# One more tile by quarters in the second column half of both feed-forward outputs, and nine DRAM sums made in another stage

## The chip, the core and the metric

The kernel runs on one core of a Trainium2 chip. The metric is the time of one execution in microseconds on the device. The engines are named as in the profile: PE (TensorE: matmuls; PEld is its weight load), DVE (VectorE), ACT (ScalarE), POOL (GpSimd) and SP (SyncE, which issues most of the DMAs).

## What is computed

One decoder layer for 512 tokens of width 1024, in float32: a half-step SwiGLU feed-forward, a token mixer (HGRN2 and mLSTM heads side by side), and a second half-step SwiGLU feed-forward, each between two RMS norms.

```python
def swiglu_ffn(x, w_in, w_out):                     # w_in 1024 x 5632, w_out 2816 x 1024
    gate, up = jnp.split(x @ w_in, 2, axis=-1)
    return (jax.nn.silu(gate) * up) @ w_out
...
x = x + 0.5 * rms_norm(swiglu_ffn(rms_norm(x, norm_pre[l, 0]), ffn1_w_in[l], ffn1_w_out[l]), norm_post[l, 0])
mixed = token_mixer(rms_norm(x, norm_pre[l, 1]), ...)
x = x + rms_norm(mixed, norm_post[l, 1])
x = x + 0.5 * rms_norm(swiglu_ffn(rms_norm(x, norm_pre[l, 2]), ffn2_w_in[l], ffn2_w_out[l]), norm_post[l, 2])
```

The change touches only how the products with `w_out` are formed, for both feed-forwards (`f1`, `f2`), and when their prepared weights are made.

## The kernel before

**Splits.** Every float32 operand of a large product is split in two rounded parts, high and low. ACT makes the high part by a copy (L294 for weights, L884 for activations), DVE the low part by a subtraction (L296, L885). A product is then three matmuls: high by high, high by low, low by high. Weights come from DRAM into the rings `raw` (3 buffers) and `raw2` (5); their split goes to one of four places (`WBUF = 4`) of the tile `w`. `feed` splits ahead for as long as a place is free; `pull` takes the next ready weight, `drop` frees its place. All items stand in one list in the order of use; a load is due up to 8 items ahead.

**Input stage of a feed-forward** (`ffn_in`). 77 products of 24 matmuls of 128 x 256 (L619), 11 tiles of 7 products, with some sums of weights made on DVE (L310; a few in the second one on POOL).

**Output stage** (`ffn_out`). The 2816 rows of `w_out` are 11 tiles `k2` of 256 rows; the 1024 output columns are two halves of 512. The loop goes over the halves, and in each over the tiles in the order `OUT`. A *plain* tile is 48 matmuls of 128 x 256 (L1004). A *quartered* tile (listed in `QUARTERED`) uses a form with seven products in place of eight: 42 matmuls (L1012), into the four accumulators `C` and four further ones `M["p1"]`, `M["p5"]`, `M["p6"]`, `M["p7"]`. Within a quartered tile the order of products is p1, C[1][1], C[1][0] (with the first weight, `w`), then p7, p5, p6, C[0][1] (with the second, `v`).

A quartered tile needs two weights: three quarters of the plain one (a split of 768 columns), and their *sums* (1024 columns), which are made beforehand in DRAM: `sums_ahead` issues three copies on SP's queue (L938 to L940) and then, one call later each, three adding transfers on POOL's queue (L944). `make_sums` advances all sums under way by one step and begins at most one new one (or up to three of those begun early).

It also needs the activations' quarters (`h_quarters`: two copies on ACT, two subtractions on DVE) and their sums (`h_sums`: three subtractions on DVE, L919), and the split of the sums (`s_tile`, into the ring `s` of three places). Tiles that are quartered in both halves keep quarters and sums from the first half; those in `TWICE` make both again in the second. Tiles 5, 7 and 9 (`APART`) share one buffer of `raw` and `gpre` for their quarters and the tile `xn` for their sums; 2, 4, 6 and 8 have places of their own in the activations' tiles `xq`, which plain tile 7 (`LATER`) uses afterwards.

After the last quartered tile of a half, `common` forms four differences from the `M` accumulators (an ACT copy, L1039, and four dependent DVE operations, L969), and `add` adds them to `C` (two DVE operations for each pair, L969 too).

**The end of the second half.** The last `LAST` tiles of the order (4 in `f1`: 0, 1, 7, 5; 2 in `f2`: 0, 1) are held back and run by chunks of 128 tokens (`chunk`, `last`). The first chunk goes tile by tile into `C[0]`, the second goes into `C[1]`, so `add(C, T, 1)` must be done before it, and `add(C, T, 0)` comes after the first. Behind each chunk its norm and residual follow.

**Where the sums of `f2` are made.** 15 sums: seven are begun at the end of `f1` (`EARLY = 7`), and these and the next six (`AHEAD = 13`) go on from calls of `make_sums` inside the mixer's jobs; the last two are made in the first half of `f2`'s output. `f1` makes its 13 sums from every fifth product of its input stage from the fifteenth on (counted from 0, behind the head products), and from every second tile of the first half.

Of the kernel before, what the change touches and what calls it, by code (L numbers as in the profile page):

```python
# [23 lines left out]
PAIRS = NF // 2  # L24
# [60 lines left out]


FIRST = (2, 3, 4, 5, 6, 7, 8, 9)
QUARTERED = {"f1": [FIRST, (2, 3, 4, 6, 8)], "f2": [FIRST, (2, 3, 4, 6, 8, 9, 5)]}
OUT = {"f1": [list(range(PAIRS)), [10, 2, 4, 3, 6, 8, 9, 0, 1, 7, 5]]}
OUT["f2"] = [OUT["f1"][0], [10, 2, 4, 3, 6, 8, 9, 5, 7, 0, 1]]  # L90
LAST, APART, TWICE = {"f1": 4, "f2": 2}, (5, 7, 9), (5, 9)
PLACES, LATER = {2: 1, 4: 2, 6: 0, 8: 3}, {7: (2, 3)}

AGAIN, ROWS = (10,), (18, 19, 20, 21)
EVERY, EARLY, AHEAD = 5, 7, 13

# [27 lines left out]
class Layer:  # L124
    def __init__(self, ctx, tc, aps):
# [717 lines left out]
    def ffn_in(self):  # L843

        nc = self.nc
        if not self.second:
            self.begun = ()
            self.sums_due("f1")
        for n, (p, t) in enumerate(ORDER2[len(HEADS2) :] if self.second else ORDER[len(HEADS) :]):
            if n > 14 and n % EVERY == 0 and not self.second:  # L850
                self.make_sums()
            if n == 14 and self.second:

                with self.behind(self.pooled):
# [12 lines left out]
        self.lag()  # L867
# [96 lines left out]
    def ffn_out(self, gpost_row, scale, after, trans, head):  # L964
# [3 lines left out]
        nc, mm = self.nc, self.nc.tensor.matmul  # L968
        tt = lambda out, a, b, op: nc.vector.tensor_tensor(out, a, b, op=op)  # L969
        f = "f2" if self.second else "f1"  # L970
        OF, QF, LF = OUT[f], QUARTERED[f], LAST[f]
        low = self.low
        seq = [(half, k2) for half in range(2) for k2 in OF[half]]
        made = deque((h, None) for h in self.hs)
# [1 line left out]
        kept, again = {}, deque()  # L976

        def more(n):
            while count[0] < min(n, len(seq)):
                half, k2 = seq[count[0]]  # L980
                count[0] += 1
                if k2 in QF[half]:
                    if k2 not in kept or half and k2 in TWICE:
                        stay = k2 in QF[1] and k2 not in TWICE
                        a = self.h_quarters(k2, PLACES.get(k2))
                        with self.behind(*([] if stay else [low])):
                            kept[k2] = a, self.h_sums(k2, stay)
                    a, f = kept[k2]
                    made.append((a, self.s_tile(f)))
                elif half and k2 in AGAIN:  # L990
                    made.append(again.popleft())
                else:
                    made.append((self.h_tile(k2, self.x_place(*LATER[k2]) if half and k2 in LATER else None), None))
                    if not half and k2 in AGAIN:
                        again.append(made[-1])

        def plain(C, w, h, i, v, begin):

            hi, lo = ([t[:, kk * 512 : (kk + 1) * 512] if len(t.shape) == 2 else t[:, kk] for kk in range(2)] for t in h)
            c = i // 2  # L1000
            out = C[i % 2][v][:, QUARTER * c : QUARTER * (c + 1)]
            for kk in range(2):
                for n, (a, b) in enumerate(((hi, 0), (hi, 1), (lo, 0))):
                    mm(  # L1004
                        out, a[kk][:, i * P : (i + 1) * P], w[:, b, kk, QUARTER * v : QUARTER * (v + 1)],
                        start=begin and c == kk == n == 0, stop=kk == 1 and n == 2, skip_group_check=True,
                    )

        def product(ps, A, B, begin):
            for c in range(2):  # L1010
                for n, (a, b) in enumerate(((0, 0), (0, 1), (1, 0))):
                    mm(  # L1012
                        ps[:, QUARTER * c : QUARTER * (c + 1)], A[a][:, c], B[b],
                        start=begin and c == n == 0, stop=n == 2, skip_group_check=True,
                    )

        def quartered(C, M, a, s, begin, early):

            quarter = lambda t, j: [self.quarters(t[:, b])[j] for b in range(2)]
            A, S = (lambda j: [a[0][j], a[1][j]]), (lambda j: [s[0][j], s[1][j]])  # L1020
            w = self.pull()
            product(M["p1"], A(1), quarter(w, 1), begin)
            product(C[1][1], A(3), quarter(w, 3), False)
            product(C[1][0], S(3), quarter(w, 2), False)
            self.drop(w)
            v, at = self.pull(), (1, 0, 2, 3)
            if early:
                product(C[0][1], A(2), quarter(v, at[3]), False)
            product(M["p7"], S(0), quarter(v, at[0]), begin)
            product(M["p5"], S(1), quarter(v, at[1]), begin)  # L1030
            product(M["p6"], S(2), quarter(v, at[2]), begin)
            if not early:
                product(C[0][1], A(2), quarter(v, at[3]), False)
            self.drop(v)

        def common(M, t):

            p1, q, x, y = t
            nc.scalar.copy(p1, M["p1"])  # L1039
            tt(q, M["p5"], p1, ALU.subtract)  # L1040
            tt(q, M["p6"], q, ALU.add)
# [12 lines left out]

        with self.behind(*([self.loaded] if self.second else [])):
            g = self.gain("gpost", gpost_row)
        if self.second:
            self.sums_due("f2", done=AHEAD)
        n = 0
        for half in range(2):  # L1060
            C = [[self.ps() for _ in range(2)] for _ in range(2)]
            M, T, left = None, None, len(QF[half])
            for m, k2 in enumerate(OF[half][: PAIRS - LF * half]):
                more(n + 2)
                h, sums = made.popleft()
                if sums:
                    begin = M is None
                    if begin:
                        M = {p: self.ps() for p in ("p1", "p5", "p7", "p6")}

                    quartered(C, M, h, sums, begin, half and OF[1][m : m + 2] == list(TWICE)[::-1])
# [135 lines left out]
    def ffn_items(self, name, w_in, w_out):  # L1207
# [570 lines left out]
    def mixer(self):  # L1778
        nc, tc = self.nc, self.tc
        self.got, self.jobs = set(), deque()  # L1780
        self.sums_due("f2", AHEAD, EARLY)
        with tc.tile_pool(name="ma", bufs=1) as ma:
            self.vh = ma.tile([P, NT, NH, P], F32, name="vh")
            self.qk = ma.tile([P, NT, T], F32, name="qk")
# [193 lines left out]
```

## Time and profile before

| What | Value |
|---|---|
| Median of 3 runs (lowest, highest) | 915.06 us (914.81, 915.23) |
| Profiled execution: own time, span | 914.82 us, 913.1 us |
| PE busy | 904.7 us (99% of the span) |
| DVE, ACT, POOL busy | 767.1, 522.3, 183.2 us |
| Mean granted PE clock | 0.999 |
| First feed-forward | from 0 to about 338 us; its output stage from about 223 |
| Mixer | to about 585 us |
| Second feed-forward: input stage, output stage | about 585 to 795, about 795 to the end |

In a group's row the columns are line, engine, operation, output and inputs, shapes and count, then busy time in us and mean ns of one, then the idle time of the engine before them and what ended it. In a timeline's row they are start and length in us, then the instruction; what stands in brackets is the engine's idle time before it and what ended it.

### The profile page before, as it was taken

What the parts mean: (1) busy time and instruction counts of PE and PEld (TensorE: products, weight loads), DVE (VectorE), ACT (ScalarE), POOL (GpSimd) and SP (SyncE); (2) the same over time, 40 slices, a digit from 0 to 9 for tenths busy, and PEclk for the clock granted to TensorE, in tenths of its full rate; (3) what the DMA queues carried; (4) which work ended last, traced back from release to release, by engine and by line L of the source; (5) the groups of instructions that cost most, each with busy time, mean ns of one, the idle gap of its engine ahead of it and who ended that gap; (6) DMA issues with size and microseconds to landing.
All of it is one profiled execution on the core that took longest, in us unless ns stands there. A gap on an engine that the chain in (4) does not pass through costs nothing.

```text
span 913.1 us, 18148 instructions
## 1 busy us (share of the span) xinstructions
PE 904.7 (99%) x7330; PEld 874.7 (96%) x7330; DVE 767.1 (84%) x1005; ACT 522.3 (57%) x749; POOL 183.2 (20%) x256
## 2 busy tenths in 40 slices
PE   9999999999999999999999999999999999999997
PEld 8999999999999999998888888899999999999997
DVE  6899988889888876699986655699899889988886
ACT  7645545557566557857643345694445545757661
POOL 2541112121111047742230300313000000010002
PEclk9999999999999999999999999999999999999999
DMA  9355779775897825899953127053354445388542
GB/s 311 83 161 140 186 191 213 188 156 137 222 273 237 249 62 143 158 200 210 204 119 116 40 76 253 24 162 95 97 156 140 139 130 156 101 238 242 171 144 93
DMA packets 127921, 146.51 MB, mean 160 GB/s; under 512 B 16335, under 2 KB 100303, under 8 KB 127837
## 3 DMA queue, kind: packets, MB, share of 16 engines
q1 hardware_dynamic: 111868, 130.14, 46.8%
q0 software_dynamic: 15680, 14.69, 11.8%
q8 instruction: 57, 0.93, 0.4%
q10 hardware_dynamic: 288, 0.52, 0.2%
q14 instruction: 28, 0.22, 0.1%
HBM read 143.20 MB, written 31.48 MB: 191 GB/s over the span
## 4 chain that ended last, share of the span: by engine, by line
PE 62%; ACT 0%; DVE 0%; DVEq 0%; POOLq 0%; issue 0%; POOL 0%; ACTq 0%
PE ps L619 23%; PE ps L1012 8%; PE ps L549 6%; PE ps L198 5%; PE ps L200 5%; PE ps L199 5%; PE ps L1004 4%; PE ps L560 1%; PE ps L1441 1%; PE ps L364 1%; PE ps L1540 0%; PE ps L1742 0%; PE ps L1491 0%; PE ps L1715 0%; PE ps L1739 0%; PE ps L1505 0%
## 5 line engine op out<-in xcount | busy, mean ns | idle before, releaser
L294 ACT CAST w<-raw 128x1024 fp32r<-128x1024 f32 x246 | 250.9, 1027 | 190.6 <-PE ps L619 91.7
L296 DVE TENSOR_TENSOR w<-raw,w 128x1024 fp32r<-128x1024 f32 x246 | 299.4, 1221 | 30.7 <-ACT w L294 29.5
L619 PE MATMUL ps<-xq,w 128*128 128x256 f32 x2016 | 236.9, 277 | 0.0
L619 PEld LDWEIGHTS ps<-xq,w 128*128 128x128 f32 x2016 | 232.8, 188 | 0.0
L619 PE MATMUL ps<-sq,w 128*128 128x256 f32 x1512 | 177.6, 276 | 0.0
L619 PEld LDWEIGHTS ps<-sq,w 128*128 128x128 f32 x1512 | 174.2, 188 | 0.0
L310 DVE TENSOR_TENSOR raw<-raw,raw 128x1024 f32<-128x1024 f32 x72 | 89.8, 1252 | 7.1 <-DMA raw<-in_ffn_w_in_dram 5.6
L1012 PE MATMUL ps<-w,hs 128*128 128x256 f32 x672 | 80.9, 276 | 0.0
L1004 PE MATMUL ps<-w,hs 128*128 128x256 f32 x672 | 79.2, 276 | 0.0
L1012 PEld LDWEIGHTS ps<-w,hs 128*128 128x128 f32 x672 | 78.3, 188 | 0.0
L1004 PEld LDWEIGHTS ps<-w,hs 128*128 128x128 f32 x672 | 77.5, 188 | 0.0
L198 PE MATMUL ps<-w,xq 128*128 128x512 f32 x176 | 71.1, 404 | 0.0
L200 PE MATMUL ps<-w,xq 128*128 128x512 f32 x176 | 68.9, 392 | 0.0
L199 PE MATMUL ps<-w,xq 128*128 128x512 f32 x176 | 68.6, 390 | 0.0
L944 POOL DMA_DIRECT2D f2sums<-in_ffn_w_out_dram x15 | 20.2, 1522 | 178.6 <-DMA f2sums<-in_ffn_w_out_dram 178.1
L549 PE MATMUL ps<-xq,w 128*128 128x256 f32 x480 | 55.7, 278 | 0.0
L549 PEld LDWEIGHTS ps<-xq,w 128*128 128x128 f32 x480 | 54.9, 188 | 0.5 <-issue 0.5
L884 ACT CAST hs<-hf 128x1024 fp32r<-128x1024 f32 x32 | 33.7, 1053 | 27.4 <-PE ps L1012 19.7
L885 DVE TENSOR_TENSOR hs<-hf,hs 128x1024 fp32r<-128x1024 f32 x32 | 39.1, 1223 | 9.0 <-ACT hs L884 8.4
L944 POOL DMA_DIRECT2D f1sums<-f1sums x26 | 22.0, 847 | 108.6 <-DMA f1sums<-in_ffn_w_out_dram 57.4
L944 POOL DMA_DIRECT2D f2sums<-f2sums x30 | 26.3, 911 | 85.7 <-DMA f2sums<-in_ffn_w_out_dram 44.6
L310 POOL TENSOR_TENSOR raw<-raw,raw 128x1024 f32<-128x1024 f32 x12 | 32.6, 2722 | 40.9 <-DVE w L296 40.7
(263 smaller groups left out, 1234.2 us busy)
## 6 DMA issues: line engine op xcount, KB each, us to landing
raw<-in_ffn_w_in_dram SPq DMA_DIRECT2D x98, 512.0 KB, 4.7
raw<-in_ffn_w_out_dram SPq DMA_DIRECT2D x44, 512.0 KB, 5.5
raw<-in_w_mix_in_dram SPq DMA_DIRECT2D x28, 512.0 KB, 4.7
raw<-f2sums SPq DMA_DIRECT2D x15, 512.0 KB, 5.1
raw<-f1sums SPq DMA_DIRECT2D x13, 512.0 KB, 6.4
raw<-in_w_mix_out_dram SPq DMA_DIRECT2D x8, 512.0 KB, 4.3
f2sums<-in_ffn_w_out_dram SPq DMA_DIRECT2D x30, 128.0 KB, 4.9
f2sums<-in_ffn_w_out_dram SPq DMA_DIRECT2D x15, 256.0 KB, 6.4
```

The lines of the kernel that those rows point to most:

```text
L198: mm(ps, sh, mh, start=start, stop=False, **kw)
L199: mm(ps, sh, ml, start=False, stop=False, **kw)
L200: mm(ps, sl, mh, start=False, stop=stop, **kw)
L294: nc.scalar.copy(hi, raw)
L296: self.low = nc.vector.tensor_tensor(lo, raw, hi.bitcast(F32), op=ALU.subtract)
L310: added = (nc.vector if late else nc.gpsimd).tensor_tensor(o, o, c, op=ALU.add)
L549: mm(ps[:, u0:u1], w[:, a, k, :], self.xop(k, b, u0, u1), start=k + n + m == 0, stop=k == ND - 1 and n == 2, skip_group_check=True,)
L619: self.nc.tensor.matmul(ps[:, c], wb[b][:, k, v], left[d][:, k, :], start=first and a + n + k == 0, stop=n == 2 and k == KH - 1, skip_grou ...
L885: self.nc.vector.tensor_tensor(lo, src, hi.bitcast(F32), op=ALU.subtract)
L944: nc.gpsimd.dma_start(to[:, a:b], v, accum_op=ALU.add)
L1004: mm(out, a[kk][:, i * P : (i + 1) * P], w[:, b, kk, QUARTER * v : QUARTER * (v + 1)], start=begin and c == kk == n == 0, stop=kk == 1 and ...
L1012: mm(ps[:, QUARTER * c : QUARTER * (c + 1)], A[a][:, c], B[b], start=begin and c == n == 0, stop=n == 2, skip_group_check=True,)
```

## The change

- In the second half, `f1` also takes tile 9 by quarters (6 quartered tiles in place of 5), and `f2` also tile 7 (8 in place of 7).
- The order of the second half becomes 10, 9, 2, 4, 3, 6, 8, 0, 1, 7, 5 in `f1` and 10, 9, 2, 5, 4, 7, 3, 6, 8, 0, 1 in `f2`. So in both the last quartered tile (8) stands directly ahead of the tiles that are held back; before, the plain tile 9 (`f1`) or 7 (`f2`) stood between.
- Tile 9's quarters and sums are kept from the first half in both. `f2` makes those of 5 and 7 again (before: 5 and 9). The rule that moved the product into C[0][1] forward when 9 and 5 were neighbours is gone.
- `f2`'s sums other than the seven early ones, now nine, are made from its own input stage, at every fifth product from the tenth on. `f1` too begins at the tenth product in place of the fifteenth, and makes 14 sums.

```diff
-QUARTERED = {"f1": [FIRST, (2, 3, 4, 6, 8)], "f2": [FIRST, (2, 3, 4, 6, 8, 9, 5)]}
-OUT = {"f1": [list(range(PAIRS)), [10, 2, 4, 3, 6, 8, 9, 0, 1, 7, 5]]}
-OUT["f2"] = [OUT["f1"][0], [10, 2, 4, 3, 6, 8, 9, 5, 7, 0, 1]]
-LAST, APART, TWICE = {"f1": 4, "f2": 2}, (5, 7, 9), (5, 9)
+QUARTERED = {"f1": [FIRST, (2, 3, 4, 6, 8, 9)], "f2": [FIRST, (2, 3, 4, 6, 8, 9, 5, 7)]}
+OUT = {"f1": [list(range(PAIRS)), [10, 9, 2, 4, 3, 6, 8, 0, 1, 7, 5]]}
+OUT["f2"] = [OUT["f1"][0], [10, 9, 2, 5, 4, 7, 3, 6, 8, 0, 1]]
+LAST, APART, TWICE = {"f1": 4, "f2": 2}, (5, 7, 9), {"f1": (), "f2": (5, 7)}
...
-            self.sums_due("f1")
+        self.sums_due(*(("f2", None, EARLY) if self.second else ("f1",)))
...
-            if n > 14 and n % EVERY == 0 and not self.second:
+            if n > 9 and n % EVERY == 0:
                 self.make_sums()
...
-                    if k2 not in kept or half and k2 in TWICE:
-                        stay = k2 in QF[1] and k2 not in TWICE
+                    if k2 not in kept or half and k2 in two:
+                        stay = k2 in QF[1] and k2 not in APART
...
-            if early:
-                product(C[0][1], A(2), quarter(v, at[3]), False)
             product(M["p7"], S(0), quarter(v, at[0]), begin)
             product(M["p5"], S(1), quarter(v, at[1]), begin)
             product(M["p6"], S(2), quarter(v, at[2]), begin)
-            if not early:
-                product(C[0][1], A(2), quarter(v, at[3]), False)
+            product(C[0][1], A(2), quarter(v, at[3]), False)
...
-        if self.second:
-            self.sums_due("f2", done=AHEAD)
...
-        self.sums_due("f2", AHEAD, EARLY)
+        self.sums_due("f2", EARLY, EARLY)
```

More of the change, by code (lines that the diff above doesn't have):

```diff
@@ L87 @@
 FIRST = (2, 3, 4, 5, 6, 7, 8, 9)
-QUARTERED = {"f1": [FIRST, (2, 3, 4, 6, 8)], "f2": [FIRST, (2, 3, 4, 6, 8, 9, 5)]}
-OUT = {"f1": [list(range(PAIRS)), [10, 2, 4, 3, 6, 8, 9, 0, 1, 7, 5]]}
-OUT["f2"] = [OUT["f1"][0], [10, 2, 4, 3, 6, 8, 9, 5, 7, 0, 1]]
-LAST, APART, TWICE = {"f1": 4, "f2": 2}, (5, 7, 9), (5, 9)
+QUARTERED = {"f1": [FIRST, (2, 3, 4, 6, 8, 9)], "f2": [FIRST, (2, 3, 4, 6, 8, 9, 5, 7)]}
+OUT = {"f1": [list(range(PAIRS)), [10, 9, 2, 4, 3, 6, 8, 0, 1, 7, 5]]}
+OUT["f2"] = [OUT["f1"][0], [10, 9, 2, 5, 4, 7, 3, 6, 8, 0, 1]]
+LAST, APART, TWICE = {"f1": 4, "f2": 2}, (5, 7, 9), {"f1": (), "f2": (5, 7)}
 PLACES, LATER = {2: 1, 4: 2, 6: 0, 8: 3}, {7: (2, 3)}
 AGAIN, ROWS = (10,), (18, 19, 20, 21)
-EVERY, EARLY, AHEAD = 5, 7, 13
+EVERY, EARLY = 5, 7
 FREE = (2, 3, 0, 1)
@@ L970, in ffn_out @@
         f = "f2" if self.second else "f1"
-        OF, QF, LF = OUT[f], QUARTERED[f], LAST[f]
+        OF, QF, LF, two = OUT[f], QUARTERED[f], LAST[f], TWICE[f]
         low = self.low
@@ L1015, in product, with quartered @@
                     )
-        def quartered(C, M, a, s, begin, early):
+        def quartered(C, M, a, s, begin):
             quarter = lambda t, j: [self.quarters(t[:, b])[j] for b in range(2)]
@@ L1069, in ffn_out @@
                         M = {p: self.ps() for p in ("p1", "p5", "p7", "p6")}
-                    quartered(C, M, h, sums, begin, half and OF[1][m : m + 2] == list(TWICE)[::-1])
+                    quartered(C, M, h, sums, begin)
                     left -= 1
```

## The prediction

> **What bounds the kernel now.** I read the page's busy shares first, then the matmul engine's waits, then the chain that ended last, and only then the order of work on DVE where the change touches it.
>
> ```profile
> span 913.1 us, 18148 instructions
> PE 904.7 (99%) x7330; PEld 874.7 (96%) x7330; DVE 767.1 (84%) x1005; ACT 522.3 (57%) x749; POOL 183.2 (20%) x256
> PE ps L194 <- POOL ones L172: 1.2, 1, 1.2
> PE ps L364 <- DVE xn L754: 0.5, 1, 0.5
> PE ps L619 <- ACT xq L384: 0.2, 1, 0.2
> ```
>
> PE is busy for 904.7 of 913.1 us, and all its listed waits together are 1.9 us. A busy PE need not be a fast one, so the chain gives the rate. Its columns are the start, the length and what ran.
>
> ```profile
> 802.81 5.44 PE ps L1004 x48
> 808.25 38.08 PE ps L1012 x336
> 846.33 10.88 PE ps L1004 x96
> 857.21 33.32 PE ps L1012 x294
> 890.53 16.33 PE ps L1004 x144
> 907.03 0.38 ACT junk L453
> ```
>
> These are the second feed-forward's output. L1004 is a plain tile of 48 matmuls, 5.44 us; L1012 a tile by quarters of 42, and eight of them take 38.08 us, 4.76 each. Both come to 0.1133 us a matmul, with no gap between tiles. So PE is packed, a matmul taken away is worth 0.1133 us, and nothing that frees another engine can give time back. The end behind the last matmul (907 to 913) is untouched. The profiled execution took 914.82 us (1.72 outside the span); the median of 915.06 lies 0.24 above it, and I apply the sum to the median.
>
> **The matmuls.** Tile 9 of the first feed-forward and tile 7 of the second go from plain to quartered in the second half: 2 x 6 x 0.1133 = 1.36 us less. By this alone 913.7. The quotient 38.08/336 is steady, so I give this term no range beyond 0.05.
>
> **What the two tiles add elsewhere.** Each brings a second weight load (512 KB) and its split, and the first one its made sum. A kept tile needs only the split of its sums, as long as the plain tile's own split. In the second feed-forward 7's quarters and sums are made again, and 9's no longer: they cancel.
>
> ```profile
> 872.75 0.92 ACT L884 CAST once<-hf 128x256 fp32r<-128x256 f32 x2
> 884.35 1.02 DVE L885 TENSOR_TENSOR once<-hf,once 128x256 fp32r<-128x256 f32 x2
> 285.44 0.95 DVE L296 TENSOR_TENSOR w<-raw,w 128x768 fp32r<-128x768 f32 x1
> 857.05:890.40 33.35, 33.35 (x297) 33.35 (x296) 27.58 (x30) 22.16 (x25) 0.00 (x0) 1.00 0.52 158
> ```
>
> The net on DVE is one split of 0.95 us per feed-forward. In the last row (length, then busy time of PE, its weight loads, DVE, ACT, POOL, then clock, DMA share, GB/s) DVE is busy 27.58 of 33.35 us: 5.8 us free, which covers it. If that cover went, each would cost at most its 0.95. Dropping the early C[0][1] product costs nothing: 9 and 5 are no longer neighbours, and tile 2's 4.76 us lies between, against the 0.92 + 1.02 us of quarters (before, they had to fit behind 9's own products).
>
> **The end of the first feed-forward's second half.** Here I see the one real price. Before, plain tile 9 stood between the last quartered tile (8) and the four tiles of the last loop (0, 1, 7, 5), and its 5.44 us covered DVE's work. After, 8 stands directly ahead of that loop.
>
> ```profile
> 309.52 8.32 PE L1004 MATMUL ps<-w,hs 128*128 128x256 f32 x72
> 319.04 2.88 PE L1004 MATMUL ps<-w,hs 128*128 128x256 f32 x24
> 310.00 1.04 ACT L294 CAST w<-raw 128x1024 fp32r<-128x1024 f32 x1
> 316.12 1.04 ACT L294 CAST w<-raw 128x1024 fp32r<-128x1024 f32 x1
> 309.23 0.68 DVE L969 TENSOR_TENSOR hf<-ps,hf 128x512 f32<-128x512 f32 x1
> 309.83 1.22 DVE L885 TENSOR_TENSOR xq<-hf,xq 128x1024 fp32r<-128x1024 f32 x1
> 310.96 0.69 DVE L969 TENSOR_TENSOR hf<-ps,hf 128x512 f32<-128x512 f32 x1
> 311.56 1.22 DVE L296 TENSOR_TENSOR w<-raw,w 128x1024 fp32r<-128x1024 f32 x1
> 314.43 0.69 DVE L969 TENSOR_TENSOR hf<-ps,hf 128x512 f32<-128x512 f32 x1
> 315.03 1.29 DVE L969 TENSOR_TENSOR ps<-ps,hf 128x512 f32<-128x512 f32 x2
> 316.25 1.23 DVE L885 TENSOR_TENSOR hs<-hf,hs 128x1024 fp32r<-128x1024 f32 x1
> 317.40 1.22 DVE L296 TENSOR_TENSOR w<-raw,w 128x1024 fp32r<-128x1024 f32 x1
> ```
>
> DVE ran without a gap from 308 to 318.6, and its last split (tile 5's weights) was done 0.5 us ahead of its use (tile 5 begins at 319.04). In a row of them a split holds DVE for 1.14 us (309.83 to 310.96) and a difference for 0.60. In the same clock, tile 8 now runs from 309.52 to 314.28. Its place for tile 7's weights frees after 18 matmuls, at 311.56; ACT starts 0.2 to 0.5 us later (before: freed 309.52, started 310.00), so DVE can take that split at about 312.85. From there it owes, before the second chunk may start: that split 1.14, four differences 2.5 (the first needs M[p5], done at 312.9), the low parts of 7 and 5 and of 5's weights 3.4 (7's low part and 5's weights lie in places that 8 holds until 314.28), and the first sum into C[1] 0.65: 7.7 us, to 320.55. PE would come there at 314.28 + 5.44 = 319.72. So 0.8 us of waiting. The best order (sums at once, x and y behind) leaves 0.4; with tile 5's low part late (needed at 318.6, done at 320.0 if a difference goes ahead of it twice) 1.4. I take 0.8, the order in which ready work is taken as in the rows.
>
> **The same place in the second feed-forward.** The last loop has two tiles, so only 24 x 0.1133 = 2.72 us cover it.
>
> ```profile
> 890.61 1.48 DVE L969 TENSOR_TENSOR hf<-ps,hf 128x512 f32<-128x512 f32 x2
> 892.13 0.69 DVE L969 TENSOR_TENSOR hf<-hf,ps 128x512 f32<-128x512 f32 x1
> 892.85 0.69 DVE L969 TENSOR_TENSOR hf<-ps,hf 128x512 f32<-128x512 f32 x1
> ```
>
> Dependent differences follow each other every 0.74 us. Tile 8 would end at 857.21 + 38.08 = 895.29, M[p5] is done 1.36 earlier, and by then DVE has finished the splits of 0 and 1 (the later place frees when 8 starts, 890.5; 0.5 + 1.04 on ACT and 1.14 on DVE end at 893.2). Four differences from 893.95 end at 896.9, the first sum into C[1] at 897.6, and PE comes for it at 898.0. Slack 0.4, so I take 0. If tile 1's low part (1.14) falls behind the differences, it is 0.7; that end stays in the range.
>
> **The nine sums.** Six leave the mixer, two leave the first half of the second feed-forward's output, and tile 7's is new; all nine are made from its input stage. Each is three copies on SP's queue and three adding transfers on POOL's.
>
> ```profile
> 340.00:585.00 245.00, 244.90 (x1570) 217.83 (x1569) 181.78 (x326) 138.78 (x206) 83.02 (x127) 1.00 0.59 143
> 60.00:230.00 170.00, 170.00 (x1499) 170.00 (x1498) 153.59 (x171) 92.47 (x117) 28.51 (x30) 1.00 0.73 183
> 600.00:795.00 195.00, 195.00 (x1719) 195.00 (x1719) 181.73 (x194) 108.82 (x140) 11.41 (x4) 1.00 0.42 127
> L944 POOL DMA_DIRECT2D f1sums<-f1sums x20: 805/812/1325, 75.5 to 224.1; - x20
> raw<-in_ffn_w_in_dram SPq DMA_DIRECT2D x28, 512.0 KB, 5.6
> raw<-in_ffn_w_in_dram SPq DMA_DIRECT2D x40, 512.0 KB, 3.6
> ```
>
> What leaves the mixer frees nothing, since PE is busy 244.90 of 245.00 us there. Where they go (600 to 795), POOL is busy 11 of 195 us and DMA at 0.42, so 27 transfers of 0.81 to 1.33 us (median and maximum of the row), 22 to 36 us on POOL, lie beside PE; what queues behind them there is nothing that PE waits for. The first feed-forward's input stage (60 to 230) already makes ten sums so, at DMA 0.73, with PE busy 170.00 of 170.00. There a weight load lands in 5.6 us against 3.6 (median): the price is 2.0 us a load. The copies stand ahead of loads on SP, which mostly waits for DVE to free a place anyhow. Is 2.0 hidden?
>
> ```profile
> 643.38 1.23 DVE L310 TENSOR_TENSOR raw<-raw,raw 128x1024 f32<-128x1024 f32 x1 [2.12 <-DMA raw<-in_ffn_w_in_dram]
> 653.20 1.22 DVE L296 TENSOR_TENSOR w<-raw,w 128x1024 fp32r<-128x1024 f32 x1
> 650.12 11.10 PE L619 MATMUL ps<-xq,w 128*128 128x256 f32 x96
> ```
>
> The stage is tightest here, behind a load that came 2.12 us late. Counting splits against products, the split at 653.20 feeds the third product of the last row (24 x 0.1133 = 2.72 each, so from 655.56), which needs the low part after 16 matmuls, at 657.4; ready at 654.4. That is 3.0 us in hand, so 2.0 more is hidden. The one sum slot more in the first feed-forward's input stage and its 14th sum go by the same rows: nothing.
>
> Sum: -1.36 + 0.8 + 0 + 0 = -0.56, to 914.5 (914.26 against the profiled execution's own 914.82).
>
> **Rivals.** *All is hidden* (25%): the low parts fall so that PE never waits; 913.7. For it: PE never waited here so far. Against: 0.5 us in hand before, with 5.44 us of cover. *The last loop's order goes badly* (12%): DVE takes the sums ahead of tile 5's low part and weights, as in the rows from 314.43 to 317.40. Then 5's weights end at 321.4 against 318.5: 2.9 us, 916.6. *The second tail waits too* (6%): 0.7 to 1.1 more, 915.4. *Weight loads starve the second input stage* (8%), which ends slower: the adding transfers and copies share the engines with the loads. It decides from a lateness of 3.0 us at 655.
>
> ```profile
> DMA to landing us min/median/max: 3.7/5.6/9.8
> ```
>
> This row is of the weight loads from 60 to 230. A load at its maximum is 9.8 - 3.6 = 6.2 us late, 3.2 over what is in hand: 914.5 + 3.2 = 917.7. Against it: in that very stage PE lost nothing. The Trainium skill ("DMA: Bandwidth & Descriptors", Queues, rings and completion order) states that each DMA engine takes turns between the queues with work, a packet at a time; a load that shares with one other queue throughout would take twice as long, an estimate of 7.2 us, and by that sum 0.6 us would show and the time be 915.1. The 5.6 us agrees in direction and is less. *A gain beyond the matmuls* (4%): 913.0, if matmuls elsewhere ran closer; no wait in the list offers it.
>
> **How the numbers follow.** The forecast (0.4 to 1.4 us lost at the first tail, 914.1 to 915.1) has 45%. The range runs from a little under the full gain to the bad order, 913.4 to 916.6, and leaves out the starving and the unexplained gain, 12%. A measurement of this kernel tells about 0.2% from no change, 1.8 us: under 913.2 is faster (5%), over 916.9 slower (the starving, and the bad order with one more loss, 11%), the rest 84%.
>
> **What the profile after would show.** L1012 has 84 matmuls more and L1004 96 fewer. Right: around 318 to 320 a PE wait on DVE (hs, w or ps L969) of about 0.8 us, none near 898, none from 640 to 795, POOL's f2sums transfers spread over that stage, weight loads there landing in 5 to 6 us. Wrong, if PE shows no wait by 320 (913.7), or waits on w or raw in the second input stage, or if the second tail's sums come later than its second chunk.

## The result, and the profile after

| | before | after |
|---|---|---|
| Median (lowest to highest) of runs beside each other | 914.81 us (914.33 to 915.23) | 923.88 us (921.82 to 924.41) |
| Ratio, 95% interval | | 1.0094, 1.008 to 1.0109 |
| Profiled execution: own time, span | 914.82, 913.1 us | 922.97, 921.3 us |

The change made the kernel 9 us slower: the forecast was 914.5, the range ended at 916.6. The profiled executions differ by 8.15 us, and these two are compared below. Lines of the page after that answer to those of before:

```profile
span 921.3 us, 18162 instructions
PE 906.4 (98%) x7318; PEld 875.7 (95%) x7318; DVE 765.9 (83%) x1007; ACT 523.6 (57%) x751; POOL 191.5 (21%) x262
L619 PE MATMUL ps<-sq,w 128*128 128x256 f32 x1512 | 179.6, 278 | 5.3 <-DVE ps L638 5.3
L310 DVE TENSOR_TENSOR raw<-raw,raw 128x1024 f32<-128x1024 f32 x72 | 89.7, 1250 | 19.7 <-DMA raw<-in_ffn_w_in_dram 18.4
```

The same two groups, and then the weight loads of the second input stage, before and after:

```profile
L619 PE MATMUL ps<-sq,w 128*128 128x256 f32 x1512 | 177.6, 276 | 0.0
L310 DVE TENSOR_TENSOR raw<-raw,raw 128x1024 f32<-128x1024 f32 x72 | 89.8, 1252 | 7.1 <-DMA raw<-in_ffn_w_in_dram 5.6
```

```profile
raw<-in_ffn_w_in_dram SPq DMA_DIRECT2D x40, 512.0 KB, 3.6
```

```profile
raw<-in_ffn_w_in_dram SPq DMA_DIRECT2D x40, 512.0 KB, 4.8
```

The 12 matmuls are gone (7330 to 7318), and yet the span is 8.2 us longer. L619 has the new wait: PE stood 5.3 us in the input stages' matmuls, waiting for the PSUM subtraction of L638 on DVE. L310 has what stood ahead of it there: the weight additions, before which DVE waited 18.4 us for loads in place of 5.6.

I set the starts of the same matmuls of both traces beside each other. The second input stage begins 0.60 us later than before and ends 8.79 later, so **8.19 us were lost in that stage**; the first feed-forward's end lost its gain (below), and the second output stage won its 0.68 with no wait, as forecast. The waits of PE in the second input stage, by the timeline (start, length, what; in brackets the idle time before):

```profile
689.80 1.98 PE L619 MATMUL ps<-xq,w 128*128 128x256 f32 x16
693.88 3.06 PE L619 MATMUL ps<-sq,w 128*128 128x256 f32 x24 [2.10 <-DVE ps L638]
...
738.54 5.60 PE L619 MATMUL ps<-xq,w 128*128 128x256 f32 x48
747.39 4.32 PE L619 MATMUL ps<-sq,w 128*128 128x256 f32 x24 [3.25 <-DVE ps L638]
751.55 2.88 PE L619 MATMUL ps<-xq,w 128*128 128x256 f32 x24
```

At 0.1133 us a matmul the product of 693.88 should have begun at 691.61 and that of 747.39 at 743.98: 2.27 and 3.41 us. Both are p6, of tiles 4 and 6; p6 adds into a place that DVE fills by subtracting from p5's result, and p5 comes only one other product earlier (2.72 us). The second wait has a tail: the 24 matmuls from 747.39 took 4.16 us in place of 2.72, at half clock. These are 7.1 of the 8.19; most of the rest, about 0.8, is a slower pace of the matmuls behind the first wait (last section).

Behind the first wait, the chain of the kernel after, in order of time, and DVE's queue over the same stretch:

```profile
675.05 7.75 DMA raw<-in_ffn_w_in_dram
...
691.90 1.22 DVE w L296
693.12 0.62 DVE ps L638
693.74 0.14 issue
693.88 8.73 PE ps L619 x72
```

```profile
682.89 1.22 DVE L310 TENSOR_TENSOR raw<-raw,raw 128x1024 f32<-128x1024 f32 x1 [4.40 <-DMA raw<-in_ffn_w_in_dram]
684.03 1.22 DVE L296 TENSOR_TENSOR w<-raw,w 128x1024 fp32r<-128x1024 f32 x1
...
690.76 1.22 DVE L310 TENSOR_TENSOR raw<-raw,raw 128x1024 f32<-128x1024 f32 x1
691.90 1.22 DVE L296 TENSOR_TENSOR w<-raw,w 128x1024 fp32r<-128x1024 f32 x1
693.04 0.69 DVE L638 TENSOR_TENSOR ps<-ps,hf 128x512 f32<-128x512 f32 x1
```

DVE stood 4.40 us for one load that took 7.75, and then worked without a gap until the subtraction at 693.04. It is not that the subtraction stood directly behind the late load: nine instructions lie between, and DVE never had the time to catch up. At the second wait of PE it is the same (the wait of 3.94 below). DVE's longest wait, at 754.93, has no wait of PE behind it:

```profile
737.24 1.23 DVE L310 TENSOR_TENSOR raw<-raw,raw 128x1024 f32<-128x1024 f32 x1 [3.94 <-DMA raw<-in_ffn_w_in_dram]
...
746.55 0.69 DVE L638 TENSOR_TENSOR ps<-ps,hf 128x512 f32<-128x512 f32 x1
...
754.93 1.22 DVE L310 TENSOR_TENSOR raw<-raw,raw 128x1024 f32<-128x1024 f32 x1 [4.83 <-DMA raw<-in_ffn_w_in_dram]
```

By 754.93 PE itself was 8.8 us behind, so the 4.83 us cost nothing more.

### The profile page after: what moved, and what is told of

Read it like the earlier page. It is cut to its first block, busy times and chain, and to the rows that moved or that the text cites. A ratio compares the mean times of both kernels' runs of the same rounds, so it can differ in the third digit from the quotient of the medians.

```text
span 921.3 us, 18162 instructions
## 1 busy us (share of the span) xinstructions
PE 906.4 (98%) x7318; PEld 875.7 (95%) x7318; DVE 765.9 (83%) x1007; ACT 523.6 (57%) x751; POOL 191.5 (21%) x262
## 3 DMA queue, kind: packets, MB, share of 16 engines
q0 software_dynamic: 16800, 15.73, 12.8%
## 4 chain that ended last, share of the span: by engine, by line
PE 45%; DVE 8%; DMA 4%; issue 4%; ACT 1%; POOL 1%; DVEq 0%; POOLq 0%; ACTq 0%
PE ps L1012 8%; PE ps L619 7%; PE ps L549 6%; PE ps L198 5%; PE ps L200 5%; PE ps L199 5%; DMA raw<-in_ffn_w_in_dram 4%; DVE w L296 4%; PE ps L1004 4%; DVE raw L310 2%; PE ps L560 1%; PE ps L1436 1%; POOL raw L310 1%; DVE ps L638 1%; PE ps L364 1%
## 5 line engine op out<-in xcount | busy, mean ns | idle before, releaser
L294 ACT CAST w<-raw 128x1024 fp32r<-128x1024 f32 (+1 forms) x248 | 252.2, 1026 | 194.5 <-PE ps L619 79.7
L296 DVE TENSOR_TENSOR w<-raw,w 128x1024 fp32r<-128x1024 f32 (+1 forms) x248 | 301.2, 1218 | 29.7 <-ACT w L294 28.2
L619 PE MATMUL ps<-xq,w 128*128 128x256 f32 x2016 | 237.2, 277 | 0.0
L619 PEld LDWEIGHTS ps<-xq,w 128*128 128x128 f32 x2016 | 233.2, 188 | 0.0
L619 PE MATMUL ps<-sq,w 128*128 128x256 f32 x1512 | 179.6, 278 | 5.3 <-DVE ps L638 5.3
L619 PEld LDWEIGHTS ps<-sq,w 128*128 128x128 f32 x1512 | 176.0, 189 | 5.8 <-issue 5.7
L310 DVE TENSOR_TENSOR raw<-raw,raw 128x1024 f32<-128x1024 f32 x72 | 89.7, 1250 | 19.7 <-DMA raw<-in_ffn_w_in_dram 18.4
L1012 PE MATMUL ps<-w,hs 128*128 128x256 f32 x720 | 86.5, 276 | 0.0
L1012 PEld LDWEIGHTS ps<-w,hs 128*128 128x128 f32 x720 | 83.8, 188 | 0.0
L944 POOL DMA_DIRECT2D f1sums<-f1sums x28 | 24.3, 868 | 111.0 <-DMA f1sums<-in_ffn_w_out_dram 54.5
L310 POOL TENSOR_TENSOR raw<-raw,raw 128x1024 f32<-128x1024 f32 x12 | 32.6, 2722 | 40.9 <-DVE w L296 40.7
L200 PEld LDWEIGHTS ps<-w,xq 128*128 128x128 f32 x176 | 33.0, 188 | 7.5 <-DVE xq L371 0.3
```

The costliest lines, as they stand in the source:

```text
L200: mm(ps, sl, mh, start=False, stop=stop, **kw)
L294: nc.scalar.copy(hi, raw)
L296: self.low = nc.vector.tensor_tensor(lo, raw, hi.bitcast(F32), op=ALU.subtract)
L310: added = (nc.vector if late else nc.gpsimd).tensor_tensor(o, o, c, op=ALU.add)
L619: self.nc.tensor.matmul(ps[:, c], wb[b][:, k, v], left[d][:, k, :], start=first and a + n + k == 0, stop=n == 2 and k == KH - 1, skip_grou ...
L944: nc.gpsimd.dma_start(to[:, a:b], v, accum_op=ALU.add)
```

## The experiments

Each kernel was timed beside the kernel before (914.46 to 915.13 in these sets). "Stage lost" below is, as above, what the second input stage lost against the profile of before by its matmuls' starts.

**Which part of the change.** The first kernel puts the second feed-forward's sums back where they were, the second moves only them.

```diff
 # the kernel after, sums as before
-        self.sums_due(*(("f2", None, EARLY) if self.second else ("f1",)))
+        if not self.second:
+            self.sums_due("f1")
...
-            if n > 9 and n % EVERY == 0:
+            if n > 9 and n % EVERY == 0 and not self.second:
...
+        if self.second:
+            self.sums_due("f2", done=13)
...
-        self.sums_due("f2", EARLY, EARLY)
+        self.sums_due("f2", 13, EARLY)
```

> The changed kernel, but the second feed-forward's sums are made where they were before (seven and six in the mixer, the last three in the first half of its own output stage). Theory 'place of the sums': the whole loss of the second input stage (8.2 us at the matmuls) comes from making nine sums there; it goes, no PE wait between 590 and 800 us, and what is left is -1.36 us for the two quartered tiles and about +1.1 us lost at the end of the first feed-forward: 914.5 us (914.0 to 915.0). Rival 'the tiles': the new order and the quartered tiles disturb the schedule wherever the sums are made; the time stays at 920 to 924 us.

```diff
 # the kernel before, only the sums moved
-            self.sums_due("f1")
+        self.sums_due(*(("f2", None, EARLY) if self.second else ("f1",)))
...
-            if n > 14 and n % EVERY == 0 and not self.second:
+            if n > (9 if self.second else 14) and n % EVERY == 0:
...
-        self.sums_due("f2", AHEAD, EARLY)
+        self.sums_due("f2", EARLY, EARLY)
```

> The kernel before, with only the place of the second feed-forward's sums changed: its eight sums other than the early seven are made from its input stage, at every fifth product from the tenth on. Theory 'place of the sums': PE waits of 2 to 4 us on DVE appear near 690 and 740 us and the time is 921 to 925 us (8 sums in place of 9; the same mechanism). Rival 'the tiles': 914.8 us, no wait.

Sums put back: 915.58 us (915.02 to 916.7), ratio 1.0009 (1.0 to 1.0018). Sums alone: 925.74 (924.82 to 927.93), ratio 1.0119 (1.0106 to 1.0133), with PE's waits on L638 at the same two products, 5.7 us in all. The place of the sums carries the loss; the quartered tiles have almost no part in it. Both times lie above what was expected: 915.58 is 0.6 over the end of its range, 925.74 is 0.7 over. In the first kernel's profiled execution the second input stage still lost 1.0 us without a listed wait of PE; nearly all of it is the slower pace of the last section.

**The second feed-forward's eighth quartered tile alone** (order and tile as in the change, sums as before, first feed-forward untouched):

```diff
-QUARTERED = {"f1": [FIRST, (2, 3, 4, 6, 8)], "f2": [FIRST, (2, 3, 4, 6, 8, 9, 5)]}
+QUARTERED = {"f1": [FIRST, (2, 3, 4, 6, 8)], "f2": [FIRST, (2, 3, 4, 6, 8, 9, 5, 7)]}
...
-OUT["f2"] = [OUT["f1"][0], [10, 2, 4, 3, 6, 8, 9, 5, 7, 0, 1]]
+OUT["f2"] = [OUT["f1"][0], [10, 9, 2, 5, 4, 7, 3, 6, 8, 0, 1]]
```

> The kernel before with only the second feed-forward's eighth quartered tile and its order (10, 9, 2, 5, 4, 7, 3, 6, 8, 0, 1), the sums made where they were; the first feed-forward as before. The forecast's second-tail term (no wait near 898): 915.0 - 0.68 = 914.3 us. If that tail waits after all: 915 to 915.5 us.

914.45 us (913.63 to 914.97), ratio 0.9993 (0.9984 to 1.0003); the last matmul comes 0.51 us sooner than in the profile of before. The 0.68 is there, and too small to be told from no change.

**Copies or adding transfers.** One kernel has the nine sets of copies in the stage and no adding transfers (they go to a spare place in DRAM; the sums are made as before). One makes the copies in the mixer, and holds the adding transfers in the stage behind a small POOL copy.

```diff
 # the kernel before, and nine sets of copies
+            if n > 9 and n % EVERY == 0 and n < 55 and self.second:
+                to = self.dram.tile([P, 4, QUARTER], F32, name=f"spare{k2}")
...
+                    nc.sync.dma_start(to[:, 0], q[:, 0, 1])
+                    nc.sync.dma_start(to[:, 1], q[:, 1, 0])
+                    nc.sync.dma_start(to[:, 2:], q[:, 1])
```

> The kernel before, with nine sets of the three copies added on SP's queue in the second input stage (into spare DRAM that nobody reads), at every fifth product from the tenth on, and no adding transfers. If copies alone make the loads late: PE waits on DVE before p6 of tiles 4 and 6, 919 to 925 us. If it takes the adding transfers: 914.5 to 916 us.

```diff
 # the kernel after, copies in the mixer, adding transfers in the stage
+                if self.second:
+                    self.mark = nc.gpsimd.tensor_copy(self.col(), self.written)
...
-            with self.behind(*([self.selected] if f == "f2" else [])):
+            with self.behind(*([getattr(self, "mark", self.selected)] if f == "f2" else [])):
...
+            self.copy_more()          # in the mixer's jobs: the three copies of one sum
```

> The changed kernel with the copies of the nine sums issued in the mixer, and the adding transfers held in the second input stage: on POOL each round of them stands behind a small copy of a column that the stage has just written, at every fifth product. If the copies on SP's queue (ahead of weight loads, 0.5 MB a sum) make the loads late, the waits at p6 go and the time is 914 to 916 us. If the adding transfers alone do it, the loss stays at half or more: 918 to 924 us.

Copies: 917.33 us (916.01 to 919.88), ratio 1.0029 (1.0019 to 1.0038). Adding transfers: 918.69 (916.58 to 920.37), 1.0038 (1.0026 to 1.0051), which is 3.1 over the kernel with the sums as before. Together they cost 8.3 (923.88 less 915.58), more than 2.3 and 3.1 added. Neither expectation holds: copies alone lie between the two ranges named for them, and the adding transfers alone are within their 918 to 924, but at 3.1 well under half of the loss.

Two earlier tries at this missed their aim. With the copies in the mixer and nothing to hold the adding transfers back, these too were ordered into the mixer; POOL waited there in order, and PE stood for 29.5 us at one place. With the copies issued on POOL's queue, POOL made them in the kernel's first 60 us, where PE's first products then waited.

```diff
 # copies early
+            self.copy_more()          # in the mixer's jobs
 # copies on POOL
+            on = nc.gpsimd if f == "f2" and not early else nc.sync
+            on.dma_start(to[:, 0], q[:, 0, 1])
```

> The changed kernel, but the three copies of each of the nine sums are issued in the mixer; only the adding transfers stay in the second input stage. 'Copies' (they stand ahead of weight loads on SP's queue, and share the DMA engines with them): weight loads land in 3.6 to 4.5 us, no PE wait in the stage, 914.5 us. 'Any transfer' (the adding transfers on POOL's queue are about half of the bytes and alone hold up the loads): about half the loss stays, 917 to 920 us.

> The changed kernel, but the copies of the nine sums made in the second input stage are issued from POOL's queue and not from SP's: the same bytes at about the same time, and no copy ahead of a weight load on SP's queue. 'Queue order' (the 1.8 us that three copies hold SP, ahead of the loads, is what makes them late): the loss goes, 914.5 us. 'Traffic' (copies and adding transfers take the engines' time while loads are under way): the loss stays, 919 to 924 us.

They took 945.39 and 926.49 us, ratios 1.0331 and 1.0134. In both, none of the nine sums' transfers is left in the second input stage; PE had no wait there, the stage lost nothing, and the loads landed in 3.7 us (median).

**The distance from p5 to p6, and the spacing of the sums.**

```diff
 # the kernel after, p5 of tiles 4, 9 and 6 moved two or three products forward
+for _t in (4, 9):
+    ORDER2.remove(("p5", _t))
+    ORDER2.insert(ORDER2.index(("p1", _t)) + 1, ("p5", _t))
-for _s, _t in ((2, 3), (6, 7), (7, 8)):
+for _s, _t in ((2, 3), (9, 6), (6, 7), (7, 8)):
```

> The changed kernel, with the product p5 of tiles 4, 9 and 6 of the second input stage moved two to four products forward, so that DVE's subtraction, which p6 starts from, has that much more time; the sums stay in the stage. Theory 'short lead': PE loses time only where p6 follows p5 by one other product (2.72 us), and weights have more in hand; with the lead the waits before p6 of 4, 9 and 6 go and the time is 914.3 to 916 us, loads as late as before. Rival 'starved': late loads hold up the weights themselves; PE then waits elsewhere in the stage (on w), 919 to 924 us.

```diff
 # the kernel after, a sum at every seventh product
-            if n > 9 and n % EVERY == 0:
+            if n > 9 and (n % 7 == 3 if self.second else n % EVERY == 0):
```

> The changed kernel with the second feed-forward's nine sums made at every seventh product of its input stage, always at the same place of a tile of seven products, in place of every fifth. The traffic is the same, spread over 7/5 of the time. Theory (lost DVE time: each load that lands late holds DVE, and the lateness adds up when the sums follow each other closely): the loss falls by more than in proportion, to 917 to 920. Rival (each set of copies and adding transfers costs what it costs, nine sets, 8.3 us, wherever they stand): 922 to 924. Second rival (only the place beside p5 and p6 counts, and seven falls onto or beside it every time): under 916, or over 925.

With p5 earlier: 920.44 us (915.88 to 925.64), ratio 1.0066 (1.0041 to 1.009). The waits at p6 of 4 and 6 were gone, but others came. Its timeline of PE (lines of the program 4 later, L623 is L619 and L642 L638):

```profile
698.41 5.72 PE L623 MATMUL ps<-sq,w 128*128 128x256 f32 x48 [1.62 <-ACT ps L674]
755.73 1.19 PE L623 MATMUL ps<-xq,w 128*128 128x256 f32 x8 [0.50 <-DVE w L300]
788.37 3.07 PE L623 MATMUL ps<-sq,w 128*128 128x256 f32 x24 [1.48 <-DVE ps L642]
```

The three stand at p3 of tile 4, p4 of tile 6 and p6 of tile 10, whose p5 was not moved; only 0.50 us is a wait for a weight (w), so neither the theory nor its rival holds. The short way from p5 to p6 is where most of the loss came out, not what made it. The times spread widely, and some 4 us of the profiled execution (923.8) were lost behind the stage, to the slower pace of the last section; so 920.44 is not a clean measure of the lead. With every seventh product: 920.36 (918.94 to 921.88), ratio 1.0063 (1.0051 to 1.0075), stage lost 4.3. Eight of the nine sets of copies and 23 of the 27 adding transfers fall in the stage here, all of them in the kernel after; this traffic, thinner, costs a little over half (4.8 against 8.3 over the kernel with the sums as before). 920.4 lies a little above the 917 to 920 of the theory and well under the 922 of its rival.

**DVE's time by itself.** The additions moved to POOL, and DVE stalled with no traffic at all:

```diff
 # the kernel after, additions of tiles 4 to 9 on POOL
-                late = out[1] >= (HEAD if out[0] == "f1" else 1)
+                late = out[1] >= (HEAD if out[0] == "f1" else 1) and (out[0], out[1]) not in ON_POOL
```

> The changed kernel with the weight additions of tiles 4 to 9 of the second input stage made on POOL in place of DVE (about 24 of 1.25 us; POOL takes 2.72 for one). Theory: the loss is DVE's queue standing behind additions that wait for a late load, so that the PSUM subtraction behind them, which the product p6 starts from, comes late. With those additions on POOL, DVE has 30 us more in the stage and does not wait there for loads: PE's waits on that subtraction go, and the time falls to 915.5 to 918. Rival: the weights themselves are late, whoever adds them. Then PE waits on w in place of the subtraction, POOL's longer additions and the adding transfers queue behind each other, and the time stays at 921 or goes above 924.

```diff
 # the kernel before, four idle reductions on DVE, of 1024, 640, 928 and 1024 columns by 4
+                        with self.behind(self.low):
+                            stall = nc.vector.tensor_reduce(
+                                self.col(4), self.xs[:, :, : STALLS[self.adds_made]], axis=mybir.AxisListType.X, op=ALU.add
+                            )
```

> The kernel before, with four DVE instructions that do nothing for the result (sums over rows of the residual) put ahead of four weight additions of the second input stage, the ones that waited longest for their loads in the changed kernel: some 4.3, 2.7, 3.9 and 4.3 us, 15 us together, against 13 us more of waiting for loads there. No transfer is added, so every load lands as before (3.6 us median). The planner knows of these four when it orders the stage. Theory one (DVE has no time to spare in this stage, so any 13 to 15 us lost there costs PE): waits of PE on the PSUM subtraction as in the changed kernel, and 919 to 924. Theory two (what costs is the lateness that the written order doesn't know of, with the subtraction standing behind it; the same time planned for is worked around): no wait over 0.5 us, 914.5 to 916.5. Rival to both (the loads and transfers themselves slow PE, DVE's waiting is only a companion): 915 and no wait either; it is told from theory two by the matmuls' pace alone.

Additions on POOL: 957.55 us (955.65 to 965.65), ratio 1.0479 (1.0451 to 1.0506), above 924 as the rival had it, though it named no such size. POOL's additions queued behind adding transfers that waited for one another. The waits of PE, of DVE and of ACT (each: us in total, times, longest; lines 1 later here):

```profile
PE ps L620 <- DVE ps L639: 30.8, 6, 10.1
PE ps L620 <- ACT w L295: 1.5, 1, 1.5
PE ps L620 <- DVE w L297: 1.2, 3, 0.6
```

```profile
DVE w L297 <- ACT w L295: 49.5, 8, 13.3
```

```profile
ACT w L295 <- POOL raw L311: 61.9, 9, 15.0
```

DVE now waited hardly for loads (3.5 us) but for ACT's splits, and ACT for weights that POOL had not added yet. Still PE's waits were on the PSUM subtraction (30.8 us), hardly on weights (2.7): whatever DVE waits for, PE feels it through what queues behind. Half of the expectation was right (the queueing on POOL, no gain), half wrong (the name of PE's wait). It doesn't tell whether DVE without that wait would have been quick enough.

The stalls alone tell more: 923.64 us (921.12 to 925.04), ratio 1.0085 (1.007 to 1.01), the loss of the whole change. Its waits, loads and timeline (lines 10 later: L629 is L619, L648 L638):

```profile
PE ps L629 <- DVE ps L648: 5.4, 2, 3.5
```

```profile
raw<-in_ffn_w_in_dram SPq DMA_DIRECT2D x40, 512.0 KB, 3.6
```

```profile
684.54 4.42 DVE L316 TENSOR_REDUCE col<-xs 128x4 f32<-128x4096 f32 x1
688.87 1.22 DVE L320 TENSOR_TENSOR raw<-raw,raw 128x1024 f32<-128x1024 f32 x1
...
694.00 0.70 DVE L648 TENSOR_TENSOR ps<-ps,hf 128x512 f32<-128x512 f32 x1
```

The loads land in 3.6 us as before, no transfer is added, and PE waits at p6 of the same tiles for the same subtraction, 5.4 us against 5.3 in the kernel after. The planner (what fixes the order of each engine's instructions before the kernel runs) knew of these four and gave DVE another order in the stage than before, and PE waits all the same; in the kernel after, whose loads come late, DVE's order there is that of before. So it isn't a matter of an order that was surprised: DVE hasn't the time. Two things stay open. The stalls came with another order, so their loss isn't that of the lost time alone; and no run kept the traffic and took DVE's waits for it away.

The kernels side by side; the second and third column are from 600 to 795 or 800 (median landing of a weight load; DVE's waits for loads, and the longest). Each row is one profiled execution, up to 1.7 us off its kernel's median, and the last column holds the half clock and the slower pace of the last section too:

| Kernel | landing | DVE waits for loads | stage lost |
|---|---|---|---|
| before | 3.6 | 5.6 (2.1) | 0 |
| after, sums as before | 3.6 | 4.6 (2.6) | 1.0 |
| copies alone | 3.7 | 7.9 (3.6) | 2.1 |
| adding transfers alone | 4.6 | 10.4 (3.2) | 5.1 |
| after, every seventh | 4.9 | 13.0 (4.3) | 4.3 |
| sums alone | 5.1 | 16.5 (7.3) | 10.5 |
| after | 4.8 | 18.4 (4.8) | 8.2 |
| before, stalls alone | 3.6 | 6.1 (2.7), and 15.6 of stalls | 10.4 |

**The first feed-forward's tail.** Three tiles held back in place of four, so that plain tile 0 covers the differences (the kernel with the sums as before otherwise):

```diff
-LAST, APART, TWICE = {"f1": 4, "f2": 2}, (5, 7, 9), {"f1": (), "f2": (5, 7)}
+LAST, APART, TWICE = {"f1": 3, "f2": 2}, (5, 7, 9), {"f1": (), "f2": (5, 7)}
```

> The changed kernel with the second feed-forward's sums made where they were before, and with three tiles held back at the first feed-forward's end in place of four, so that plain tile 0 stands between quartered tile 8 and the held-back tiles 1, 7, 5. Theory: the two waits at that end (0.4 near 319 on hs, 0.6 more near 338.5 on w) come from DVE's and ACT's splits standing behind the differences of the last quartered tile. With 5.44 us more of cover the first one goes and with it the queue that makes the second: both quartered tiles then give their 0.68 each, 913.7 to 914.1. Rival one: only the wait near 319 goes and the one near 338.5 stays, since it hangs on the places of the next weights: 914.3 to 914.6. Rival two: the first tail's cost has nothing to do with the cover, and the time is that of the kernel with only the place of the sums put back, 915.4 to 915.8.

918.96 us (918.04 to 919.94), ratio 1.0046 (1.0033 to 1.0059): outside all three. The wait near 319 is gone as the theory had it, but a chunk now has three tiles of matmuls in place of four, and these no longer cover the norms of the chunk before:

```profile
336.38 1.32 PE L364 MATMUL ps<-ident,hf 128*128 128x128 f32 x8 [1.06 <-DVE hf L481]
...
340.47 5.76 PE L560 MATMUL ps<-xq,w 128*128 128x256 f32 x48 [0.70 <-ACT xq L370]
...
348.31 0.63 PE L364 MATMUL ps<-ident,xn 128*128 128x128 f32 x4 [1.18 <-DVE xn L481]
```

By the second input stage it is 5.2 us behind; 1.8 of it came only in the mixer, from 349 to 406, where the matmuls ran at the slower pace of the last section. No kernel tried is measurably faster than the one before.

## Why the prediction was wrong, point by point

**Matmuls, -1.36: right.** The second tail's 0.68 shows whole; the first one's was there and spent.

**The first tail, +0.8: the place and the mechanism right, the size in two parts.** Timeline of PE after:

```profile
318.54 0.84 PE L1004 MATMUL ps<-w,hs 128*128 128x256 f32 x6
319.65 2.90 PE L1004 MATMUL ps<-w,hs 128*128 128x256 f32 x23 [0.27 <-DVE hs L885]
...
339.54 5.73 PE L560 MATMUL ps<-xq,w 128*128 128x256 f32 x48 [0.71 <-ACT w L294]
```

PE waited for tile 5's low part (hs) near 319.5, as the worse order of that step had it; the six matmuls of 318.54 end their issue at 319.22, so 0.43 us. What the step didn't have is a second wait at 339.54, on ACT's split of the mixer's first weight: 0.71 us, and by the matmuls' starts 0.63 more than stood there before. Together 1.1, so that the tile's gain of 0.68 became a loss of about 0.4. Why ACT's split comes later there wasn't tried.

**The second tail, 0: right.** No wait near 898.

**The nine sums, 0: wrong.** The step that failed is "That is 3.0 us in hand, so 2.0 more is hidden." It put the term at nothing; the runs put it at 8.3 us (923.88 less 915.58). Its three parts fell one by one.

The stretch from 643 to 657, called the tightest, lies almost wholly ahead of the traffic. In the kernel after, SP issues the stage's first copy here:

```profile
655.26 0.51 SPq L938 DMA_DIRECT2D f2sums<-in_ffn_w_out_dram  x1
```

Behind it DVE is nearly as full. Its busy time in the kernel before, from 661 to 691 (length; busy time of PE, its weight loads, DVE, ACT, POOL; clock, DMA share, GB/s), and its one wait there:

```profile
661.00:691.00 30.00, 30.00 (x266) 30.00 (x266) 28.39 (x30) 15.40 (x20) 0.00 (x0) 1.00 0.47 141
```

```profile
679.63 1.23 DVE L310 TENSOR_TENSOR raw<-raw,raw 128x1024 f32<-128x1024 f32 x1 [1.54 <-DMA raw<-in_ffn_w_in_dram]
```

DVE is busy 28.39 of 30 us, and 1.54 of the other 1.61 is one wait for a load. In the kernel after the same addition waits 4.40 (at 682.89), 2.86 more, and at the end of just this stretch PE loses 2.27. And 3.0 us was the lead of one weight, while what came late was a subtraction for which nothing had been counted: the step asked who waits for the load, not what is queued behind the instruction that waits. So the prediction's own sign of being wrong, waits of PE on w or raw in that stage, named the wrong wait too: PE's were on ps.

The 2.0 was a difference of medians. The median after rose by only 1.2 us (3.6 to 4.8), but single loads took 7.75 and 6.85, and DVE's longest wait 4.8.

The first feed-forward's input stage was taken as proof that the traffic is harmless. DVE's waits there, and in the second one (before, from 60 to 230 and from 600 to 795; us in total, times, longest):

```profile
DVE ps L638 <- PE ps L619: 11.0, 10, 1.4
DVE w L296 <- ACT w L294: 3.5, 12, 0.5
```

```profile
DVE raw L310 <- DMA raw<-in_ffn_w_in_dram: 5.6, 3, 2.1
DVE hf L638 <- PE ps L619: 2.5, 3, 1.3
DVE ps L638 <- PE ps L619: 2.1, 3, 0.9
```

In the first stage DVE waits ten times for PE, and no wait for a load is listed: it is ahead. In the second it waits 5.6 us for loads and 4.6 for PE: it is ahead only in part. That this is why the first stage bears the traffic is read from these rows; no run tried it.

The rival "weight loads starve the second input stage" had the place and the sign, at 8% and 917.7. It priced one load at its latest against the weight's lead; late loads at three additions (DVE's waits of 4.40, 2.69 and 3.94) with DVE full between them gave 8.2 us. The margin of DVE comes nearer: 195 less 181.7 busy less 5.6 of waits leaves 7.7 us over the stage, against 12.8 us of waits more (18.4 less 5.6). The 5.1 that it doesn't cover is about the 5.3 of PE's listed waits; the half clock and the slower pace come on top. This is worked out behind the result, and no second case tests it.

The Trainium skill ("DMA: Bandwidth & Descriptors", Queues, rings and completion order) has each DMA engine take turns between the queues with work, and from that and the measured 3.6 comes the estimate of 7.2 us for a load that shares the engines with one other queue throughout. The latest loads (7.75, 6.85) come near it, the median of 4.8 doesn't.

## What to carry to other kernels

Before a step is called hidden, look on the engine that will wait for it: what that engine has free in the same 30 us, and what queues behind the waiting instruction, count for more than the lead of the item that is late. A stage that bears a traffic well is evidence only for stages whose helper engine is ahead in the same way; the list of its waits is a first sign (waits for PE: ahead; waits for loads: behind). To tell late data from a lack of an engine's time, stall that engine alone, with no traffic.

## What the runs showed of the hardware that was not expected

**A slower pace at the full granted clock.** Durations of the single matmuls of L619 in the kernel after from 694.5 to 715 and in the kernel before from 690 to 714 (ns: least, median, most):

```profile
L619 PE MATMUL ps<-sq,w x93: 281/281/282, 694.3 to 713.6; 128*128 128x256 f32 x93
```

```profile
L619 PE MATMUL ps<-sq,w x107: 276/276/277, 691.0 to 714.0; 128*128 128x256 f32 x107
```

With it the distance from matmul to matmul goes from 113.3 to 117.9 ns (48 in 5.66 us from 699.60 in place of 5.44), for some 20 us after the wait of 2.1, while the clock's rows stay at 1.00. That is about 0.8 us on top of the wait. After the half clock below the pace was 113.3 again. It isn't a matter of a long wait. The kernel with the sums as before has it from 662 to 680 behind a matmul that started 0.2 us late, with no listed wait, and the kernel with p5 earlier has it behind a wait of 1.48 from 788 to its last matmuls (L1016 is L1012); behind waits of 1.56 (copies alone) and of 1.81 and 1.60 (every seventh) the matmuls stayed at 276 ns:

```profile
L619 PE MATMUL ps<-sq,w x91: 281/281/281, 662.7 to 679.0; 128*128 128x256 f32 x91
```

```profile
L1016 PE MATMUL ps<-w,once x144: 281/281/281, 818.8 to 894.3; 128*128 128x256 f32 x144
```

The cause is open.

**Half clock behind some waits, and not by their length alone.** The kernel after from 740 to 750, the kernel with the stalls alone from 690 to 700, and the adding transfers alone from 745 to 750:

```profile
740.00:750.00 10.00, 6.75 (x49) 6.59 (x48) 9.43 (x10) 2.22 (x3) 1.17 (x1) 0.84 0.81 179
```

```profile
690.00:700.00 10.00, 6.53 (x36) 6.33 (x35) 8.16 (x10) 2.68 (x3) 0.00 (x0) 0.69 0.40 113
```

```profile
745.00:750.00 5.00, 5.00 (x32) 5.00 (x31) 3.19 (x4) 0.97 (x2) 0.00 (x0) 0.66 0.79 203
```

The granted clock fell to a mean of 0.84, 0.69 and 0.66 in these slices, behind waits of 3.25, 3.47 and 1.92 us; behind the waits of 2.10 (after, the first one), 1.81 and 1.60 (every seventh) and 1.56 (copies alone) it stayed at 1.00. The Trainium skill ("TensorE: Matmul & The Clock Gate", Part 1) has the clock halved after an idle window of about 3.4 us. The waits of 3.25 and 3.47 us are near that, the one of 1.92 isn't, and the measurement decides.
